# A ConvFFN's start on one core: pair sums in place, six leading products, earlier weight loads

## The chip, the cores and the metric

The kernel runs on one core of one Trainium2 chip. The metric is the device time of one execution in microseconds; of the kernel before there are three runs and one profiled execution.

## The reference

The reference is one decoder layer on a sequence of 1024 tokens of width 1024, in float32: sparse attention with a token indexer, then a gated ConvFFN, both with adaLN shift, scale and gate, and a last RMSNorm. The part that matters here:

```python
x = x + gt_m * y                                  # y: attention's output @ w_o
h = rmsnorm(x, g_ffn[i]) * (1 + sc_f) + sh_f
u, v = jnp.split(h @ w_in, 2, axis=-1)            # w_in: 1024 x 5632
u = causal_depthwise_conv(u, conv_w) + conv_b     # width 3
x = x + gt_f * ((gelu(u) * v) @ w_out)            # w_out: 2816 x 1024
```

## The kernel before, in words

TensorE (PE) multiplies in fp32r, so each operand is split into a high part (a cast on ACT) and a low part (a subtraction on DVE or POOL), `split` (L122), and each product is three matmuls, `three` (L126). The line of nearly all instructions in the profile is L89, the helper that issues them; the reader goes by tile names.

*Output projection* (L1277 to L1293, tiles `ot`, `wo`, `xt`). The attention's output, `o_sb`, lies in eight tiles of 128 tokens. In round r, `w0(r)` (L1064) transposes tile r (`ot`) and splits it (`o_h`, `o_l`); `w1(r-1)` (L1077) multiplies the tile before with the eight splits of `w_o` (48 matmuls into one accumulator of 1024 columns, `wo`), adds the result to `x` (tile `xr`, DVE), stores it (`x1d`) and normalizes it (`norm`, L221: a square on ACT, `rx` on DVE, a power on POOL, then `xn` on the engine that `NW`, L62, names). `w2a(r-2)` (L1100) transposes `xn` (`xt`) and applies the FFN's scale and shift, giving `hm`: on ACT in eight pieces for tiles 3, 6, 7 (`HM_ACT`, L64), on DVE for the others. `w2b(r-2)` (L1115) splits two of the seven combinations that the products use, `b11` and `s4` for tiles 0 to 3, `b22` and `s3` for tiles 4 to 7: a half of `hm`, and the difference `diff` of its halves (both `comb`). `W2B_DVE` (L63) names the low parts that DVE computes; POOL does the others.

In the same rounds `w_sums` (L1249) loads pairs of rows of `f_w_out` (`wb`), makes four sums and one scaling with `gt_f` on DVE (five operations of 128 x 512) and stores four results (`wt`) for the down products. `T_AT` (L69) says how many of the eleven pairs each round does.

*Up products.* Both FFN matrix products are done by halves with seven products in place of eight (`prods`, L1142 ff.). For each of 22 chunks c of 128 columns, product i = 0 to 6 has 12 matmuls of 512 columns; on the weights' side it takes a block of `f_w_in` or a sum of two blocks, on the other side `s4`, `b11` (these need tokens 0 to 511), `b22`, `s3` (tokens 512 to 1023), `s1`, `s7`, `s6` (sums of a tile of the first half and one of the second). The weights are loaded by SP (`load_up`, L1134, tile `fw`, two halves j of 512 KB per chunk), summed on POOL into one of two `ring` buffers (`prep_sum`, L1154) and split into `pr` (`prep_split`, L1164; the low part on POOL, for product 3 on DVE). `after` (L1184) combines the accumulators `m` into `u` and `v` on ACT and DVE.

*Between the two.* PSUM is first a pool of four accumulators of 1024 columns; it is closed after tile 7's `w1` (L1294), and a pool of eight accumulators of 512 columns (`banks`) takes its place. Then come tile 6's transposes, product (0,0), (0,1), tile 7's transposes, (1,0), (1,1); in between, the pair sums of s1, s7, s6 are made tile by tile (`sum_tile`, L1303, 24 sums of 128 x 256) into tiles of their own, and then split (`sum_split`, L1312, six splits of 128 x 1024).

*What sets the order.* From L559 on the program's order is a priority only: Tile's scheduler orders each engine's queue at build time by its own timing model, and an instruction that is ready goes ahead of one that is not. At run time each queue, SP's of DMAs too, is worked in that order. SBUF tiles of 4 KB a partition come from 35 slots (`NSLOT`, L29): a load or a result waits for a free one. In the loop over products `steps` (L1374) asks for sums two products ahead and splits one ahead, and `run_plan` (L1369) for the loads of chunk c + 1 at position 7c + `LOAD_AT` (L65).

Of the kernel before, what the change touches and what calls it, by code (L numbers as in the profile page):

```python
# [24 lines left out]
NF = DFF // P  # L25
# [34 lines left out]
CUT_7 = 2  # L60
FREE = "AGD"
NW = 'PDDDPPDD'  # L62
W2B_DVE = {(6, 1), (4, 1), (5, 1), (6, 0)}  # L63
HM_ACT = (3, 6, 7)  # L64
LOAD_AT = (3, 3)  # L65
UP_LOW_DVE = ((3,), (3, 6))
D_ORDER = (1, 2, 5, 6, 3, 7, 4)
D_LOAD, D_SPLIT = 16.0, 7.0
T_AT = (2, 2, 2, 1, 1, 1, 1, 1)  # L69
FIN_LAG = (1.3, 0.3)  # L70


def body(ctx, tc, a):
# [39 lines left out]
    def bank1(name):  # L113
        return bank2(name)[:, :512]
# [959 lines left out]
        ost[t] = o_h, o_l  # L1074
        split(o_h, o_l, pt.rearrange("p (k t) -> p k t", k=KD), dve)

    def w1(t):  # L1077
        o_h, o_l = ost[t]
        ps = bank2("wo")
        for j in range(2):  # L1080
            js = slice(j * 512, (j + 1) * 512)
            for k in range(KD):
                three(ps[:, js], o_h[:, k], o_l[:, k], wo[k][0][:, js], wo[k][1][:, js], k == 0, k == KD - 1)
        x1 = x_r[t]
        dve.tensor_tensor(x1, ps, x1, op=OP.add)
        nc.sync.dma_start(x1d[t], x1)
        xn1[t] = norm(x1, NW[t])

# [11 lines left out]
    def w2a(t, halves):  # L1100

        hf, o = divmod(t, 4)
        hm[t] = g = slot([P, KD, P], F, f"hm{t}")
        for k in range(KD):
            pe.transpose(halves[k // 4][:, k % 4], xn1[t][:, k * P:(k + 1) * P], ident)
        if t in HM_ACT:
            for k in range(KD):
                act.activation(g[:, k], halves[k // 4][:, k % 4], AF.Identity, bias=sh_f[:, k:k + 1], scale=a_f[:, k:k + 1])
        else:
            for i in range(2):  # L1110
                ks = slice(4 * i, 4 * i + 4)
                dve.tensor_tensor(g[:, ks], halves[i], bc(ada["a_f"][:, ks]), op=OP.mult)
            dve.tensor_tensor(g, g, bc(sh_f), op=OP.add)
# [132 lines left out]

    wt = {(i, d): dram.tile([2, P, 512], F, name=f"wt{i}_{d}") for i in range(4, 8) for d in range(ND)}

    def w_sums(q):  # L1249
        b1, b2 = [slot([P, D], F, f"wb{c}") for c in range(2)]  # L1250
        for c, b in enumerate((b1, b2)):
            nc.sync.dma_start(b, a["f_w_out"][(2 * q + c) * P:(2 * q + c + 1) * P])
        for i, o, x, y, op in ((5, b1[:, lo_t], b1[:, hi_t], b1[:, lo_t], OP.subtract),
                               (7, b1[:, hi_t], b2[:, hi_t], b1[:, hi_t], OP.subtract),
                               (6, b2[:, hi_t], b2[:, hi_t], b1[:, lo_t], OP.subtract),
# [12 lines left out]
    def on_pe(dur, f):  # L1268
# [3 lines left out]
        f()  # L1272
        clock[0] += dur

    comb_big(("b11", "s4"))
    comb_big(("b22", "s3"))
    for r in range(NT):  # L1277
        w0(r)
        if r == NT - 2:
            load_up(0, 1)  # L1280
        if r == NT - 1:
            ring = slot([P, 2, 4, P], F, "ring")
            prep_split(0, 0)
            prep_sum(0, 1)
            prep_split(0, 1)
        if r >= 1:
            w1(r - 1)
        if r >= 2:
            w2a(r - 2, [bank1("xt").rearrange("p (k t) -> p k t", k=4) for _ in range(2)])
            w2b(r - 2)  # L1290
        for q in range(sum(T_AT[:r]), sum(T_AT[:r + 1])):
            w_sums(q)
    w1(NT - 1)  # L1293
    psum_ctx.close()  # L1294
    banks = ctx.enter_context(tc.tile_pool(name="banks", bufs=8, space=bass.MemoryType.PSUM))

    def two_banks():
        return [bank("xt").rearrange("p (k t) -> p k t", k=4) for _ in range(2)]

    sums = {}  # L1300
    terms = {"s1": (0, 4), "s7": (4, 4), "s6": (0, 0)}

    def sum_tile(nm, o):  # L1303
        if o == 0:
            sums[nm] = [slot([P, 2, 512], F, f"{nm}s{i}") for i in range(2)]
        sl = slice(o * P, (o + 1) * P)
        x, y = terms[nm]
        for i in range(2):
            dve.tensor_tensor(sums[nm][i][:, :, sl], hm[o][:, x + 2 * i:x + 2 * i + 2],
                              hm[4 + o][:, y + 2 * i:y + 2 * i + 2], op=OP.add)  # L1310

    def sum_split(nm):  # L1312
        h, lo = [], []
        for i in range(2):
            h.append(slot([P, 2, 512], R, f"{nm}h{i}"))
            lo.append(slot([P, 2, 512], R, f"{nm}l{i}"))
            act.copy(h[i], sums[nm][i])
            dve.tensor_tensor(lo[i], sums[nm][i], h[i].bitcast(F), op=OP.subtract)
        comb[nm] = (lambda k: h[k // 2][:, k % 2]), (lambda k: lo[k // 2][:, k % 2])

    load_up(1, 1)
    w2a(NT - 2, two_banks())
    product(0, 0)
    load_up(0, 0)
    prep_sum(1, 1)
    prep_split(1, 0)
    w2b(NT - 2)
    prep_split(1, 1)
    prep_sum(0, 2)
    for nm in ("s1", "s7"):  # L1330
        for o in range(2):
            sum_tile(nm, o)
    product(0, 1)
    w2a(NT - 1, two_banks())
    product(1, 0)
    after(0, 1)
    w2b(NT - 1)
    prep_split(0, 2)
    prep_split(0, 3)
    prep_sum(0, 4)  # L1340
    for nm in ("s1", "s7"):
        for o in range(2, 4):
            sum_tile(nm, o)
    product(1, 1)
    sum_split("s1")
    after(1, 1)
    prep_split(0, 4)
    prep_sum(0, 5)
    for o in range(4):
        sum_tile("s6", o)  # L1350
    sum_split("s7")
    prep_split(0, 5)
    prep_sum(0, 6)
    sum_split("s6")
    prep_split(0, 6)
    seq = [(0, i) for i in range(2, 7)] + [(1, i) for i in range(2, 7)]
    seq += [(c, i) for c in range(2, NF) for i in range(7)]
    prepared = {(0, i) for i in range(7)} | {(1, 0), (1, 1)}
    summed = set(prepared)
    loaded = {(0, 0), (0, 1), (1, 1)}  # L1360

    plan = []
    for c in range(NF):
# [259 lines left out]
```

## Time and profile before

| what | value |
|---|---|
| three runs | 1184.88, 1187.29, 1187.45 us; median 1187.29 |
| the profiled execution | 1190.08 us |
| its span, first to last instruction | 1188.3 us |
| mean granted TensorE clock | 0.971 |
| output projection | about 424 to 523 us of the span |
| up products | 528 to 971 us |
| down products | to 1180 us |

Times in the profile are microseconds from the first instruction of one execution. PE is TensorE's matmuls, PEld its weight loads, DVE VectorE, ACT ScalarE, POOL GpSimd, SP the queue that issues DMAs. A row of a timeline gives start, duration, engine, operation, tiles (out<-in), shape, how many were merged, and in brackets the idle time before and what ended it.

### The profile page before, as it was taken

What the parts mean: (1) busy time and instruction counts of PE and PEld (TensorE: products, weight loads), DVE (VectorE), ACT (ScalarE), POOL (GpSimd) and SP (SyncE); (2) the same over time, 40 slices, a digit from 0 to 9 for tenths busy, and PEclk for the clock granted to TensorE, in tenths of its full rate; (3) what the DMA queues carried; (4) which work ended last, traced back from release to release, by engine and by line L of the source; (5) the groups of instructions that cost most, each with busy time, mean ns of one, the idle gap of its engine ahead of it and who ended that gap; (6) DMA issues with size and microseconds to landing.
All of it is one profiled execution on the core that took longest, in us unless ns stands there. A gap on an engine that the chain in (4) does not pass through costs nothing.

```text
span 1188.3 us, 15292 instructions
## 1 busy us (share of the span) xinstructions
PE 1108.0 (93%) x5419; PEld 914.9 (77%) x5419; DVE 897.8 (76%) x1367; ACT 540.9 (46%) x909; POOL 619.3 (52%) x379
## 2 busy tenths in 40 slices
PE   7899599869999999987999999999999999999997
PEld 6787488756777787875878887888788888888885
DVE  6867489779887659789768776887678786555587
ACT  2376578656544622334434333333334355343352
POOL 2453023032144623448989998999899840200353
PEclk8899799979999999998999999999999999999999
DMA  9633201001655579851033323323242449975351
GB/s 364 219 127 54 53 18 55 1 1 31 211 170 188 177 274 333 293 186 54 36 106 106 116 81 98 133 89 95 84 133 89 147 154 369 390 250 179 104 195 71
DMA packets 69432, 173.30 MB, mean 146 GB/s; under 512 B 6472, under 2 KB 8936, under 8 KB 69352
## 3 DMA queue, kind: packets, MB, share of 16 engines
q1 hardware_dynamic: 69208, 172.04, 42.9%
q8 instruction: 42, 0.69, 0.2%
q14 instruction: 38, 0.31, 0.1%
q10 hardware_dynamic: 144, 0.26, 0.1%
HBM read 130.59 MB, written 41.68 MB: 145 GB/s over the span
## 4 chain that ended last, share of the span: by engine, by line
PE 52%; DVE 8%; POOL 5%; DMA 5%; issue 3%; ACT 2%; SPq 0%; POOLq 0%; DVEq 0%; ACTq 0%
PE m L89 24%; PE d L89 18%; PE o L89 3%; PE wo L89 3%; DMA fw<-in_f_w_in 3%; POOL pr L89 3%; PE l L89 2%; DVE wb L89 2%; POOL ring L89 2%; PE pt L89 1%; DMA wb<-in_f_w_out 1%; DVE conv L89 1%; DVE xr L89 1%; DVE lg L89 0%; DMA ada<-in_ada_w 0%
## 5 line engine op out<-in xcount | busy, mean ns | idle before, releaser
L89 PE MATMUL m<-comb,pr 128*128 128x512 f32 x1056 | 252.3, 395 | 12.2 <-ACT comb L89 5.3
L89 PEld LDWEIGHTS m<-comb,pr 128*128 128x128 f32 x1056 | 200.4, 191 | 57.3 <-ACT pr L89 6.0
L89 PE MATMUL d<-ringb,ringa 128*128 128x512 f32 x888 | 202.1, 389 | 0.0
L89 POOL TENSOR_TENSOR pr<-ring,pr 128x512 fp32r<-128x512 f32 x108 | 190.7, 1780 | 19.6 <-ACT pr L89 19.4
L89 PEld LDWEIGHTS d<-ringb,ringa 128*128 128x128 f32 x888 | 166.7, 188 | 34.6
L89 POOL TENSOR_TENSOR ring<-fw,fw 128x512 f32<-128x512 f32 x66 | 117.4, 1791 | 1.8
L89 POOL TENSOR_TENSOR y<-y,gt_f 128x512 f32<-128x512 f32 x12 | 23.6, 1985 | 156.5 <-DVE y L89 156.5
L89 ACT CAST pr<-ring 128x512 fp32r<-128x512 f32 x110 | 66.7, 618 | 67.7 <-POOL ring L89 67.5
L89 DVE SCALAR_TENSOR_TENSOR conv<-u,small,conv 128x1023 f32<-128x1023 f32 (+1 forms) x44 | 66.8, 1518 | 28.2 <-ACT conv L89 26.8
L89 DVE TENSOR_TENSOR ringa<-da,ringa 128x1024 fp32r<-128x1024 f32 (+1 forms) x40 | 49.0, 1225 | 51.3 <-ACT ringa L89 51.1
L89 DVE TENSOR_TENSOR u<-m,u 128x512 f32<-128x512 f32 x66 | 45.3, 687 | 51.2 <-PE m L89 34.8
L89 ACT CAST ringa<-da 128x1024 fp32r<-128x1024 f32 (+1 forms) x40 | 39.6, 989 | 90.5 <-PE d L89 78.5
L89 ACT ACTIVATE lg<-lg,mx 128x128 f32<-128x128 f32 (+6 forms) x64 | 49.5, 775 | 47.8 <-DVE mx L89 47.3
L89 PEld LDWEIGHTS o<-vv,ptb 128*128 128x128 f32 x528 | 64.4, 192 | 7.5 <-issue 4.8
L89 PE MATMUL l<-kt,q 128*128 128x512 f32 (+3 forms) x160 | 66.9, 533 | 2.9 <-ACT ptb L89 1.4
L89 POOL TENSOR_TENSOR ring<-fw 128x512 f32<-128x512 f32 x44 | 61.0, 1385 | 15.8 <-DMA fw<-in_f_w_in 15.6
L89 PE MATMUL o<-vv,ptb 128*128 128x128 f32 x528 | 66.9, 276 | 0.0
L89 PE MATMUL m<-s7h,pr 128*128 128x512 f32 x176 | 58.0, 391 | 1.3 <-POOL pr L89 1.3
L89 PE MATMUL m<-s6h,pr 128*128 128x512 f32 x176 | 59.0, 396 | 0.0
L89 PE MATMUL m<-s1h,pr 128*128 128x512 f32 x176 | 58.0, 390 | 0.3 <-POOL pr L89 0.3
L89 POOL TENSOR_TENSOR mn<-near,score 128x1024 f32<-128x1024 f32 x12 | 29.8, 2487 | 51.2 <-PE pt L89 16.5
L89 ACT ACTIVATE conv<-u,small 128x1024 f32<-128x1024 f32 x22 | 27.4, 1244 | 59.3 <-DVE u L89 59.3
(294 smaller groups left out, 2591.5 us busy)
## 6 DMA issues: line engine op xcount, KB each, us to landing
fw<-in_f_w_in SPq DMA_DIRECT2D x44, 512.0 KB, 4.9
da<-ga SPq DMA_DIRECT2D x35, 512.0 KB, 6.8
ada<-in_ada_w SPq DMA_DIRECT2D x32, 512.0 KB, 3.9
wb<-in_f_w_out SPq DMA_DIRECT2D x22, 512.0 KB, 5.6
wt<-wb SPq DMA_DIRECT2D x44, 256.0 KB, 2.1
db<-wt SPq DMA_DIRECT2D x20, 512.0 KB, 9.4
ga<-conv SPq DMA_DIRECT2D x33, 256.0 KB, 2.1
db<-in_f_w_out SPq DMA_DIRECT2D x15, 512.0 KB, 6.4
```

The costliest lines, as they stand in the source:

```text
L89: r = f(*args, **kw)
```

## The change

Seven edits around the start of the FFN. Both low parts of tile 7 go from POOL to DVE (`W2B_DVE`). The eleven pairs of `f_w_out` are done in rounds 0 to 5 (`T_AT`) and loaded one round ahead (`w_load`). `w1` adds and accumulates by halves of 512 columns, tile 7's in an order by k, and the transposes of the tile before it stand in the middle of `w1(6)` and of `w1(7)`; the PSUM pools are switched before `w1(7)`, and the transposes of a tile take one accumulator of the first pool, not two. Tile 7's `hm` is half on DVE. The pair sums are made in place in `hm` (`w2c`, three sums of 128 x 512 per tile, for tiles 0 and 1 within rounds 6 and 7) and split from there tile by tile (`w2d`). Six products, (c,0) and (c,1) of chunks 0, 1 and 2, precede the first that needs tile 7, and the order after them is new (`seq`). The loads of chunk c + 1 are asked for at positions 7c - 1 and 7c (`LOAD_AT`).

```diff
--- before.py
+++ after.py
@@ -60,13 +60,13 @@
 CUT_7 = 2
 FREE = "AGD"
 NW = 'PDDDPPDD'
-W2B_DVE = {(6, 1), (4, 1), (5, 1), (6, 0)}
+W2B_DVE = {(6, 1), (4, 1), (5, 1), (6, 0), (7, 0), (7, 1)}
 HM_ACT = (3, 6, 7)
-LOAD_AT = (3, 3)
+LOAD_AT = (-1, 0)
 UP_LOW_DVE = ((3,), (3, 6))
 D_ORDER = (1, 2, 5, 6, 3, 7, 4)
 D_LOAD, D_SPLIT = 16.0, 7.0
-T_AT = (2, 2, 2, 1, 1, 1, 1, 1)
+T_AT = (2, 2, 2, 2, 2, 1)
 FIN_LAG = (1.3, 0.3)
 
 
@@ -1074,15 +1074,19 @@
         ost[t] = o_h, o_l
         split(o_h, o_l, pt.rearrange("p (k t) -> p k t", k=KD), dve)
 
-    def w1(t):
+    def w1(t, halves, between=None):
+
+
         o_h, o_l = ost[t]
-        ps = bank2("wo")
-        for j in range(2):
+        jk = [(j, k) for j in range(2) for k in range(KD)]
+        x1 = x_r[t]
+        for n, (j, k) in enumerate(sorted(jk, key=lambda e: e[1]) if t == NT - 1 else jk):
+            if between and n == KD:
+                between()
             js = slice(j * 512, (j + 1) * 512)
-            for k in range(KD):
-                three(ps[:, js], o_h[:, k], o_l[:, k], wo[k][0][:, js], wo[k][1][:, js], k == 0, k == KD - 1)
-        x1 = x_r[t]
-        dve.tensor_tensor(x1, ps, x1, op=OP.add)
+            three(halves[j], o_h[:, k], o_l[:, k], wo[k][0][:, js], wo[k][1][:, js], k == 0, k == KD - 1)
+            if k == KD - 1:
+                dve.tensor_tensor(x1[:, js], halves[j], x1[:, js], op=OP.add)
         nc.sync.dma_start(x1d[t], x1)
         xn1[t] = norm(x1, NW[t])
 
@@ -1104,7 +1108,11 @@
         for k in range(KD):
             pe.transpose(halves[k // 4][:, k % 4], xn1[t][:, k * P:(k + 1) * P], ident)
         if t in HM_ACT:
-            for k in range(KD):
+            on_dve = 4 if t == NT - 1 else 0
+            if on_dve:
+                dve.tensor_tensor(g[:, 0:4], halves[0], bc(ada["a_f"][:, 0:4]), op=OP.mult)
+                dve.tensor_tensor(g[:, 0:4], g[:, 0:4], bc(sh_f[:, 0:4]), op=OP.add)
+            for k in range(on_dve, KD):
                 act.activation(g[:, k], halves[k // 4][:, k % 4], AF.Identity, bias=sh_f[:, k:k + 1], scale=a_f[:, k:k + 1])
         else:
             for i in range(2):
@@ -1246,10 +1254,15 @@
 
     wt = {(i, d): dram.tile([2, P, 512], F, name=f"wt{i}_{d}") for i in range(4, 8) for d in range(ND)}
 
+    w_raw = {}
+
+    def w_load(q):
+        w_raw[q] = [slot([P, D], F, f"wb{c}") for c in range(2)]
+        for c, b in enumerate(w_raw[q]):
+            nc.sync.dma_start(b, a["f_w_out"][(2 * q + c) * P:(2 * q + c + 1) * P])
+
     def w_sums(q):
-        b1, b2 = [slot([P, D], F, f"wb{c}") for c in range(2)]
-        for c, b in enumerate((b1, b2)):
-            nc.sync.dma_start(b, a["f_w_out"][(2 * q + c) * P:(2 * q + c + 1) * P])
+        b1, b2 = w_raw[q]
         for i, o, x, y, op in ((5, b1[:, lo_t], b1[:, hi_t], b1[:, lo_t], OP.subtract),
                                (7, b1[:, hi_t], b2[:, hi_t], b1[:, hi_t], OP.subtract),
                                (6, b2[:, hi_t], b2[:, hi_t], b1[:, lo_t], OP.subtract),
@@ -1272,8 +1285,36 @@
         f()
         clock[0] += dur
 
+    def two_banks():
+        t = bank2("xt").rearrange("p (h k t) -> p h k t", h=2, k=4)
+        return [t[:, 0], t[:, 1]]
+
+    def w2c(o):
+
+        g0, g1 = hm[o], hm[4 + o]
+        dve.tensor_tensor(g0[:, 4:8], g0[:, 4:8], g1[:, 4:8], op=OP.add)
+        dve.tensor_tensor(g1[:, 0:4], g1[:, 0:4], g0[:, 0:4], op=OP.add)
+        dve.tensor_tensor(g0[:, 0:4], g0[:, 0:4], g1[:, 4:8], op=OP.add)
+
+    parts = {}
+
+    def w2d(nm, o):
+
+        if nm not in parts:
+            parts[nm] = h, lo = [[slot([P, 2, 512], R, f"{nm}{x}{i}") for i in range(2)] for x in "hl"]
+            comb[nm] = (lambda k: h[k // 2][:, k % 2]), (lambda k: lo[k // 2][:, k % 2])
+        h, lo = parts[nm]
+        sl = slice(o * P, (o + 1) * P)
+        t, x = {"s1": (o, 0), "s7": (o, 4), "s6": (4 + o, 0)}[nm]
+        for i in range(2):
+            src = hm[t][:, x + 2 * i:x + 2 * i + 2]
+            act.copy(h[i][:, :, sl], src)
+            dve.tensor_tensor(lo[i][:, :, sl], src, h[i][:, :, sl].bitcast(F), op=OP.subtract)
+
     comb_big(("b11", "s4"))
     comb_big(("b22", "s3"))
+    for q in range(T_AT[0]):
+        w_load(q)
     for r in range(NT):
         w0(r)
         if r == NT - 2:
@@ -1283,81 +1324,63 @@
             prep_split(0, 0)
             prep_sum(0, 1)
             prep_split(0, 1)
+            load_up(1, 1)
         if r >= 1:
-            w1(r - 1)
+            ps = bank2("wo")
+            w1(r - 1, [ps[:, :512], ps[:, 512:]], (lambda: w2a(r - 2, two_banks())) if r == NT - 1 else None)
         if r >= 2:
-            w2a(r - 2, [bank1("xt").rearrange("p (k t) -> p k t", k=4) for _ in range(2)])
+            if r < NT - 1:
+                w2a(r - 2, two_banks())
             w2b(r - 2)
         for q in range(sum(T_AT[:r]), sum(T_AT[:r + 1])):
             w_sums(q)
-    w1(NT - 1)
+        for q in range(sum(T_AT[:r + 1]), sum(T_AT[:r + 2])):
+            w_load(q)
+        if r >= 6:
+            w2c(r - 6)
     psum_ctx.close()
     banks = ctx.enter_context(tc.tile_pool(name="banks", bufs=8, space=bass.MemoryType.PSUM))
 
     def two_banks():
         return [bank("xt").rearrange("p (k t) -> p k t", k=4) for _ in range(2)]
 
-    sums = {}
-    terms = {"s1": (0, 4), "s7": (4, 4), "s6": (0, 0)}
-
-    def sum_tile(nm, o):
-        if o == 0:
-            sums[nm] = [slot([P, 2, 512], F, f"{nm}s{i}") for i in range(2)]
-        sl = slice(o * P, (o + 1) * P)
-        x, y = terms[nm]
-        for i in range(2):
-            dve.tensor_tensor(sums[nm][i][:, :, sl], hm[o][:, x + 2 * i:x + 2 * i + 2],
-                              hm[4 + o][:, y + 2 * i:y + 2 * i + 2], op=OP.add)
-
-    def sum_split(nm):
-        h, lo = [], []
-        for i in range(2):
-            h.append(slot([P, 2, 512], R, f"{nm}h{i}"))
-            lo.append(slot([P, 2, 512], R, f"{nm}l{i}"))
-            act.copy(h[i], sums[nm][i])
-            dve.tensor_tensor(lo[i], sums[nm][i], h[i].bitcast(F), op=OP.subtract)
-        comb[nm] = (lambda k: h[k // 2][:, k % 2]), (lambda k: lo[k // 2][:, k % 2])
-
-    load_up(1, 1)
-    w2a(NT - 2, two_banks())
-    product(0, 0)
+    w1(NT - 1, [bank("wo") for _ in range(2)], lambda: w2a(NT - 2, two_banks()))
+    load_up(2, 1)
     load_up(0, 0)
+    w2b(NT - 2)
     prep_sum(1, 1)
     prep_split(1, 0)
-    w2b(NT - 2)
+    w2c(2)
     prep_split(1, 1)
-    prep_sum(0, 2)
-    for nm in ("s1", "s7"):
-        for o in range(2):
-            sum_tile(nm, o)
+    load_up(1, 0)
+    product(0, 0)
     product(0, 1)
+    after(0, 1)
     w2a(NT - 1, two_banks())
     product(1, 0)
-    after(0, 1)
+    prep_split(2, 0)
+    prep_sum(2, 1)
+    prep_split(2, 1)
     w2b(NT - 1)
+    product(1, 1)
+    after(1, 1)
+    prep_sum(0, 2)
     prep_split(0, 2)
     prep_split(0, 3)
-    prep_sum(0, 4)
-    for nm in ("s1", "s7"):
-        for o in range(2, 4):
-            sum_tile(nm, o)
-    product(1, 1)
-    sum_split("s1")
-    after(1, 1)
-    prep_split(0, 4)
-    prep_sum(0, 5)
+    w2c(3)
     for o in range(4):
-        sum_tile("s6", o)
-    sum_split("s7")
-    prep_split(0, 5)
-    prep_sum(0, 6)
-    sum_split("s6")
-    prep_split(0, 6)
-    seq = [(0, i) for i in range(2, 7)] + [(1, i) for i in range(2, 7)]
-    seq += [(c, i) for c in range(2, NF) for i in range(7)]
-    prepared = {(0, i) for i in range(7)} | {(1, 0), (1, 1)}
+        w2d("s1", o)
+    product(2, 0)
+    product(2, 1)
+    after(2, 1)
+    for nm in ("s7", "s6"):
+        for o in range(4):
+            w2d(nm, o)
+    seq = [(c, i) for c in range(2) for i in (2, 3)] + [(c, i) for c in range(2) for i in (4, 5, 6)]
+    seq += [(2, i) for i in range(2, 7)] + [(c, i) for c in range(3, NF) for i in range(7)]
+    prepared = {(c, i) for c in range(3) for i in range(2)} | {(0, 2), (0, 3)}
     summed = set(prepared)
-    loaded = {(0, 0), (0, 1), (1, 1)}
+    loaded = {(c, j) for c in range(2) for j in range(2)} | {(2, 1)}
 
     plan = []
     for c in range(NF):
```

## Rows read from the trace of the kernel before

**Rows 1.** The page's first part: busy time, share of the span and instructions of each engine
```profile
PE 1108.0 (93%) x5419; PEld 914.9 (77%) x5419; DVE 897.8 (76%) x1367; ACT 540.9 (46%) x909; POOL 619.3 (52%) x379
```

**Rows 2.** Windows by stage: engines' busy us (x instructions), granted clock, DMA share, GB/s
```profile
424.00:523.20 99.20, 97.04 (x472) 80.92 (x470) 78.88 (x101) 24.80 (x42) 37.74 (x23) 1.00 0.77 278
523.20:605.00 81.80, 67.85 (x271) 53.73 (x271) 68.05 (x77) 37.40 (x62) 63.99 (x37) 0.90 0.25 85
605.00:971.50 366.50, 363.64 (x1600) 299.40 (x1599) 286.74 (x269) 143.12 (x212) 332.40 (x204) 1.00 0.34 111
971.50:1180.00 208.50, 208.50 (x921) 172.35 (x920) 138.59 (x140) 87.41 (x110) 44.44 (x30) 1.00 0.61 216
...
610.00:700.00 90.00, 90.00 (x399) 74.38 (x398) 65.97 (x65) 34.54 (x52) 82.90 (x53) 1.00 0.32 103
```

**Rows 3.** The timeline of PE, 523 to 605 us: the products that PE waited for
```profile
526.42 1.95 PE L89 MATMUL xt<-ident,xn 128*128 128x128 f32 x8 [3.01 <-DVE xr L89]
...
546.78 4.45 PE L89 MATMUL m<-comb,pr 128*128 128x512 f32 x11 [5.35 <-ACT comb L89]
...
553.47 4.36 PE L89 MATMUL m<-comb,pr 128*128 128x512 f32 x11 [2.24 <-POOL comb L89]
...
562.37 0.73 PE L89 MATMUL m<-s7h,pr 128*128 128x512 f32 x2 [1.29 <-POOL pr L89]
...
600.69 0.73 PE L89 MATMUL m<-comb,pr 128*128 128x512 f32 x2 [1.79 <-ACT pr L89]
```

**Rows 4.** Windows over the four stretches at the lower clock: one, and their sum
```profile
543.50:550.50 7.00, 3.72 (x9) 2.96 (x10) 7.00 (x15) 5.34 (x7) 3.70 (x1) 0.51 0.00 0
...
sum 17.90, PE 14.20 PEld 11.54 DVE 12.56 ACT 11.41 POOL 11.14; mean PE 3.55 PEld 2.88 DVE 3.14 ACT 2.85 POOL 2.79
```

**Rows 5.** The timeline of DVE and of ACT, tiles 6 and 7
```profile
525.15 1.22 DVE L89 TENSOR_TENSOR xr<-wo,xr 128x1024 f32<-128x1024 f32 x1
...
528.45 0.75 DVE L89 TENSOR_SCALAR xn<-xr,rxr 128x1024 f32<-128x1024 f32 x1 [0.66 <-POOL rxr L89]
...
531.82 4.72 DVE L89 TENSOR_TENSOR s1s<-hm,hm 128x256 f32<-128x256 f32 x4
...
545.39 0.68 DVE L89 TENSOR_TENSOR diff<-hm 128x512 f32<-128x512 f32 x1
...
536.96 1.54 ACT L89 ACTIVATE hm<-xt,sh_f,a_f 128x128 f32<-128x128 f32 x4
```

**Rows 6.** The timeline of POOL, 527 to 554 us
```profile
527.87 0.55 POOL L89 TENSOR_TENSOR rxr<-rx,mhalf 128x1 f32<-128x1 f32 x1 [9.24 <-DVE rx L89]
...
531.82 1.58 POOL L89 TENSOR_TENSOR ring<-fw 128x512 f32<-128x512 f32 x1 [3.40 <-DMA fw<-in_f_w_in]
...
546.80 6.61 POOL L89 TENSOR_TENSOR comb<-diff,comb 128x512 fp32r<-128x512 f32 x1 [4.56 <-ACT comb L89]
```

**Rows 7.** Instructions of tiles hm, ot and wb: duration ns min/median/max
```profile
L89 DVE TENSOR_TENSOR s1s<-hm,hm x8: 408/415/1519, 531.8 to 546.0; 128x256 f32<-128x256 f32 x8
...
L89 DVE TENSOR_TENSOR s6s<-hm,hm x8: 406/408/408, 549.5 to 551.9; 128x256 f32<-128x256 f32 x8
...
L89 DVE TENSOR_TENSOR o_l<-ot,o_h x8: 1208/1224/1225, 422.6 to 504.4; 128x1024 fp32r<-128x1024 f32 x8
...
L89 DVE TENSOR_TENSOR wb<-wb x22: 678/685/1660, 425.0 to 523.8; 128x512 f32<-128x512 f32 x22
```

**Rows 8.** The output projection: a wait of PE; windows of two stretches
```profile
448.77 0.47 PE L89 MATMUL wo<-woh,o_h 128*128 128x512 f32 x1 [1.54 <-DVE xr L89]
...
431.90:442.20 10.30, 10.30 (x47) 8.51 (x47) 2.61 (x4) 2.05 (x3) 3.43 (x2) 1.00 0.62 212
...
473.00:486.00 13.00, 13.00 (x69) 10.97 (x68) 12.57 (x16) 3.31 (x5) 4.42 (x3) 1.00 0.78 284
```

**Rows 9.** The waits of 572 to 966 us: us in total, times, longest
```profile
ACT pr L89 <- DMA fw<-in_f_w_in: 41.6, 17, 5.2
...
PE m L89 <- ACT pr L89: 4.3, 3, 1.8
```

## The prediction

> **What bounds the kernel now.** I read the page first: PE is busy 93% of the span, DVE 76%, POOL 52% [rows 1]. The averages hide the stages, so windows by stage come next [rows 2]. The output projection (424 to 523.2 us) is idle on PE for 99.20 - 97.04 = 2.2 us; the down products (971.5 to 1180) for nothing; the up products from 605 on for 366.50 - 363.64 = 2.9 us, with POOL busy 332 of 366 us, so POOL is close behind PE there. The stage between, 523.2 to 605, is the weak one: PE idles 13.95 us and the granted clock is 0.90. An undisturbed stretch (610 to 700) has 399 products in 90 us, 0.2256 us each. The weak stage holds 271 instructions, 255 of them products (57.5 us), and 16 transposes (some 2 us): 59.5 us of work in 81.8. **22.3 us are lost there.** The timeline of PE names the waits [rows 3]: 3.01 us for DVE's add of tile 7 (`xr`), 5.35 for ACT's and 2.24 for POOL's split of tile 7's difference, 1.29 for a weight split on POOL, 1.79 for one on ACT. The clock is at its lower level, 1.2 GHz, in four stretches that follow the waits of 3.01, 5.35, 2.24 and 1.79 us; in these PE is busy 14.20 us at about half pace [rows 4], which costs 7.1. The rest of the 22.3, 1.3 us, goes in restarts.
>
> Why was tile 7 late? Its `hm` was done on ACT by 536.96 + 1.54 = 538.5, but DVE's subtraction `diff` ran at 545.39, behind pair sums [rows 5]. Four of these, of 256 columns, took 4.72 us together [rows 5]: alone one takes 0.41 us, at worst 1.52 [rows 7]. The dear ones are those that meet POOL's work; an operation with one input in PSUM (`o_l`) never stretches, 1.21 to 1.23 us [rows 7]. POOL's side of the same meeting is the 6.61 us for one split, where an operation of that size took 1.58 before it [rows 6]. POOL meanwhile stood idle for 9.24 us, 3.40 (waiting for a weight load) and 4.56 us [rows 6].
>
> **The change, part by part.** T is the end of the last output product, today 523.2.
>
> *Switch of PSUM pools.* Today the transposes of tile 6, the new pool's first users, wait for tile 7's add, which DVE starts at 525.15 behind the last pair of `f_w_out`. Now the switch lies between `w1(6)` and `w1(7)`, and the add is in halves. The wait that is left is for the second half: at least 0.6 us (half of 1.22 [rows 5]), at most today's 3.01. The nearest row is the 1.54 us that a product waited for the same add [rows 8], after which the clock stayed up (1.00 in that window [rows 2]). I take 1.3.
>
> *Six products as cover.* Tile 7's add takes 0.7 us; from its end to `xn` ready took 2.83 today (526.37 to 529.20 [rows 5]): T+3.6. PE reaches tile 7's transposes after two products, T+5.4, and ends them at T+6.4. Half of `hm` is then on ACT (four pieces, 1.54 [rows 5]), half in two operations on DVE (two of 0.69 [rows 7]): T+8. Cast, subtraction, cast and two subtractions on DVE follow: 2.6 us alone, 5 when each meets POOL: T+10.6 to T+13. The first product that needs them, (0,2), comes after six products and the transposes, at T+17.2 (6 x 12 x 0.2256 + 1). The margin of 4 to 7 us covers even today's delay of `diff` (545.39 - 538.5 = 6.9) nearly. The waits of 5.35 and 2.24 and their slow stretches go; I count 0, and what is late next is POOL.
>
> *POOL's supply.* Products (2,0) and (2,1) add three POOL operations, some 5 us, ahead of (0,2). Against that stand 17 us of idleness and 5 us of the long split [rows 6], which moves to DVE with the other half of tile 7. The loads of chunks 1 and 2 are asked for earlier, but SP issues them in order, behind `x1d` stores that wait for DVE. Of 1.29 + 1.79 us and the clock behind the latter I leave 2.0 us (between 0 and 5).
>
> *Pair sums in place, splits by tile.* Out: 24 sums of 256 columns and 6 wide splits; in: 12 sums of 512 (6 of them before T) and 24 casts on ACT with 24 subtractions of 256 on DVE. The casts, at least 0.38 us each (1.54 / 4 [rows 5]), 9 us or more, lie on ACT, busy 37 of 82 us in this stage [rows 2]. Alone, DVE has 24 x 0.41 + 6 x 1.21 = 17.1 us before, 12 x 0.69 + 24 x 0.41 = 18.1 after (a 512 takes 0.69 [rows 7]); 1 us more, beside PE. Meeting POOL, each small subtraction costs 1.5. They are due from T+28 ((0,4), after ten products). Those of tiles 0 to 2 need nothing of tile 7 and can run while POOL waits. I take 4 us of waiting, nearer to the lower end, since POOL's idle stretches [rows 6] lie where these operations can start; ends 0 and 32 (worked out as a rival).
>
> The Trainium skill (SBUF — State Buffer, "SBUF: two separate sides") states that DVE with two inputs in SBUF and GpSimd exclude each other for a whole instruction; the 0.41 against 1.52 us and the steady `o_l` agree. By that rule alone all 24 pay, the slower case below. The skill's Perfetto Trace Analysis ("Optimizing Scalar/DVE Operations") gives some 60 ns of overhead per DVE operation on SBUF and advises grouping; by it 18 more operations cost 1.1 us, my estimate, while the rows here give 6 x (4 x 0.41 - 1.21) = 2.6.
>
> The stage keeps 1.3 + 2.0 + 4.0 = 7.3 us of its 22.3: **15.0 us gained.**
>
> *The output projection.* A pair of `f_w_out` costs DVE five operations of 0.69, 3.5 us. T_AT moves the pairs of rounds 6 and 7 into rounds 3 and 4. DVE was busy 12.57 of 13 us there [rows 8], so it runs 3 us over in each; queued behind it are the adds, `o_l` and `xn`, and PE waits for these. On the other side loads a round ahead use a stretch in which DVE worked 2.61 of 10.30 us [rows 8], transposes take one PSUM tile where they took two, and half of a tile's add now runs beside PE. The adds as halves cost DVE 8 x (2 x 0.69 - 1.22) = 1.3 us, beside PE. **Gain 1.0**, between 2.2 (all idle time gone) and a loss of 6. The loads and stores of a moved pair, 2 MB, come on top of a DMA share of 0.78 there [rows 8]; SP issues them between the stores of `x1d`, so they can delay those.
>
> *LOAD_AT.* Loads of chunk c+1 are issued at position 7c-1 and 7c, not 7c+3: 4 and 3 products, 11 and 8 us, earlier, for two more slots. ACT waited 41.6 us for these loads, but PE only 4.3 for ACT [rows 9], 1.79 of it counted above; 2.9 us of idleness is left after 605. **Gain 2.0** (0 to 2.9).
>
> **Sum.** 15.0 + 1.0 + 2.0 = 18.0. The profiled execution took 1190.08 us (span 1188.3 and 1.8 around it), which gives 1172.1; it is 2.8 above the median of the runs, 1187.29, so the median after is **1169 us**.
>
> **Rivals.**
> A, slower: **DVE in step with POOL.** From about T+6 POOL works without a break. In program order 12 operations on SBUF (`w2c`, `w2b(7)`, `hm`, two weight splits) and s1's 8 come first: 20 x 1.5 + 5 us on PSUM = T+41, 13 us after (0,4) is due. s7's and s6's 8 each take 12 us against 2.7 us of product: 9 us each. That is 31 us of idleness and some 5 us of clock in place of my 4: 32 lost against 18 gained, 1201. Every small subtraction done before POOL starts saves 1.5, so it decides at 12 of 24: fewer, and the kernel is slower. Half way to the full case: 1194. For it: 4.72 us for four sums. Against: the 8 sums of s6 ran at 0.41 each [rows 7]; the worst is no rule.
> B: **the projection paced by DVE.** The two overfull rounds are not absorbed: 6 us lost and the gain of 1 gone, 1169 + 7 = 1176. For: 12.57 of 13. Against: the idle stretch before it [rows 8].
> C: **the loads do not come ahead.** 35 slots are shared; sixteen hold `w_o` until T and eight `hm`, so asking earlier may issue nothing earlier, and the change would not do what it says. Then the 2.0 of LOAD_AT goes, POOL waits for chunk 2 as it waited 3.40 us [rows 6], and the supply costs 5 to 8 instead of 2: 1169 + 2 + 6 = 1177. Against: pairs of `f_w_out` leave the last rounds, which frees slots.
>
> **How the numbers follow.** Forecast 0.55, A 0.14, B 0.18, C 0.13. A measurement here tells 0.2%, 2.4 us, from no change. The forecast and nearly all of B and C are faster by more than that (0.55 + 0.16 + 0.11 = 0.82); 0.05 falls within; 0.13 is slower. The lower end: with the switch at 0.6, nothing else left in the stage, 2.2 and 2.9 from the others, 26.8 gained, 1160.5; all at once is unlikely, so 1162. The upper end takes in B, C with worse supply, and the bound of A: 1187.
>
> **What would show it.** Right: a wait of 0.6 to 1.6 us on PE at `w1(7)`'s first product and none at tile 6's transposes; six products (s4, b11) from T without a gap; `diff` of tile 7 done before T+17; no 6.6 us operation on POOL; fewer us of ACT waiting for `fw`; 523 to 605 at a clock near 1. Wrong: products of s1, s7, s6 waiting for DVE after T+28 with subtractions of 1.5 us (A); waits for `xr` or `o_l` in 450 to 500 (B); `fw` issued no earlier against its products (C). A gap elsewhere, in the down products above all, would contradict the whole account.

## The result: 0.8% slower, and the profile after

The changed kernel takes 1195.14 us (median of 8 runs, 1192.48 to 1201.56), the kernel before 1186.09 in the runs beside it: ratio 1.0079, 95% interval 1.0060 to 1.0097, some 9 us slower where 18 faster was forecast. The profiled execution took 1195.40 us (span 1193.6), 5.3 longer than that of before; the other 4 us are mostly that the profiled execution of before lay 2.8 to 4 us above its medians. The spans divide like this (us; from the first and the last row of a tile in each trace):

| stretch | before | after |
|---|---|---|
| start to the first output product (`wo`) | 422.6 | 423.3 |
| first to last output product | 100.8 | 114.1 |
| to the last up product (`m`) | 447.9 | 439.6 |
| to the last down product (`d`) | 209.2 | 209.2 |
| rest | 7.8 | 7.4 |

The FFN's start gained 8.3 us, and the output projection lost 13.3. By the page's first part the averages hardly differ from [rows 1]:

```profile
PE 1110.1 (93%) x5419; PEld 914.7 (77%) x5419; DVE 894.5 (75%) x1385; ACT 540.1 (45%) x923; POOL 608.6 (51%) x377
```

The windows by stage of the changed kernel (columns as in [rows 2]) show where the time is, and the last row the end of the projection at a lower clock:

```profile
423.30:537.40 114.10, 103.81 (x492) 83.95 (x491) 87.09 (x120) 29.43 (x52) 39.29 (x24) 0.99 0.71 256
537.40:620.00 82.60, 71.15 (x289) 55.76 (x289) 68.00 (x83) 35.57 (x69) 58.99 (x37) 0.94 0.25 80
620.00:977.00 357.00, 356.30 (x1572) 294.84 (x1571) 278.48 (x266) 140.20 (x209) 324.69 (x201) 1.00 0.33 111
977.00:1186.20 209.20, 209.20 (x922) 172.67 (x920) 139.34 (x140) 87.42 (x110) 44.42 (x30) 1.00 0.62 217
508.40:537.40 29.00, 26.06 (x116) 20.88 (x114) 17.77 (x24) 9.43 (x20) 15.76 (x9) 0.94 0.15 55
```

PE now idles 114.10 - 103.81 = 10.3 us in the projection, where it idled 2.2 [rows 2]. The timeline of PE there names the waits:

```profile
432.21 0.50 PE L89 MATMUL wo<-woh,o_h 128*128 128x512 f32 x1 [1.71 <-DVE xr L89]
...
445.19 0.51 PE L89 MATMUL wo<-woh,o_h 128*128 128x512 f32 x1 [0.78 <-DVE xr L89]
...
460.34 0.50 PE L89 MATMUL wo<-woh,o_h 128*128 128x512 f32 x1 [0.41 <-DVE xr L89]
...
472.59 1.09 PE L89 MATMUL xt<-ident,xn 128*128 128x128 f32 x8 [1.08 <-DVE xn L89]
...
474.87 0.50 PE L89 MATMUL wo<-woh,o_h 128*128 128x512 f32 x1 [0.31 <-DVE xr L89]
...
487.31 1.09 PE L89 MATMUL xt<-ident,xn 128*128 128x128 f32 x8 [1.23 <-DVE xn L89]
...
501.10 0.51 PE L89 MATMUL wo<-woh,o_h 128*128 128x512 f32 x1 [0.82 <-DVE xr L89]
...
514.43 1.09 PE L89 MATMUL xt<-ident,xn 128*128 128x128 f32 x8 [0.34 <-POOL xn L89]
517.24 0.80 PE L89 MATMUL wo<-woh,o_h 128*128 128x512 f32 x1 [1.72 <-DVE xr L89]
...
525.35 0.47 PE L89 MATMUL wo<-woh,o_h 128*128 128x512 f32 x1 [0.88 <-DVE xr L89]
```

Count the products between two such rows: the waits for `xr` stand after the 24th product of a tile, not after the 48th. At 432.21, 445.19, 460.34, 474.87, 501.10 and 517.24 PE wants to begin the second half of tiles 0, 1, 2, 3, 5 and 6, and waits until DVE has added the first: 5.75 us. In the gaps of tiles 3, 4 and 6 stand transposes, which wait for `xn` themselves (2.65 us); tile 4 has no wait for `xr` behind them. Two waits for `o_l` take 1.02, and the switch of PSUM pools, the last row, 0.88: 10.3 in all. That is 8.1 us more idleness than before. The other 5 us of the 13.3 are mostly tile 6's transposes, which moved in (0.9), restarts (the first product after a wait takes 0.50 us, others 0.39), and slow clock behind the 1.72 (the 24 products there took 7.24 us, those behind the 0.82 took 5.70).

After T (now 537.4) the waits of 5.35, 2.24 and 3.01 us [rows 3] are gone, and these stand in their place:

```profile
544.64 1.09 PE L89 MATMUL xt<-ident,xn 128*128 128x128 f32 x8 [1.82 <-DVE xn L89]
...
558.81 4.85 PE L89 MATMUL m<-comb,pr 128*128 128x512 f32 x20 [1.24 <-DVE pr L89]
565.19 0.73 PE L89 MATMUL m<-comb,pr 128*128 128x512 f32 x2 [1.52 <-ACT pr L89]
...
568.59 3.96 PE L89 MATMUL m<-comb,pr 128*128 128x512 f32 x10 [1.67 <-POOL pr L89]
...
613.31 11.33 PE L89 MATMUL m<-comb,pr 128*128 128x512 f32 x36 [4.08 <-ACT pr L89]
```

The timelines of POOL, ACT and DVE show two in-order queues behind them. ACT casts for s7 and s6, sixteen in a row (5.1 us), and POOL stands 8.20 us for a cast of `pr` queued behind them:

```profile
565.21 3.32 POOL L89 TENSOR_TENSOR pr<-ring,pr 128x512 fp32r<-128x512 f32 x1 [8.20 <-ACT pr L89]
...
559.61 2.55 ACT L89 CAST s7h<-hm 128x256 fp32r<-128x256 f32 x8
562.06 2.55 ACT L89 CAST s6h<-hm 128x256 fp32r<-128x256 f32 x8
564.52 0.61 ACT L89 CAST pr<-ring 128x512 fp32r<-128x512 f32 x1
...
564.65 2.76 DVE L89 TENSOR_TENSOR s6l<-hm,s6h 128x256 fp32r<-128x256 f32 x8
```

Some 40 us later DVE has the first four sums for the down products (`sa`, `sb`), three of them at 1.6 to 1.8 us beside POOL, ahead of `u` and `v` of chunk 2; ACT's `conv` of chunk 2 waits 11.27 us for `u`, and the casts of chunk 3 wait behind it:

```profile
602.17 1.59 DVE L89 TENSOR_TENSOR sa<-conv 128x512 f32<-128x512 f32 x1
603.68 1.77 DVE L89 TENSOR_TENSOR sb<-conv 128x512 f32<-128x512 f32 x1
605.38 1.77 DVE L89 TENSOR_TENSOR sa<-sa,conv 128x512 f32<-128x512 f32 x1
607.08 0.68 DVE L89 TENSOR_TENSOR u<-m,u 128x512 f32<-128x512 f32 x1
...
611.51 1.24 ACT L89 ACTIVATE conv<-u,small 128x1024 f32<-128x1024 f32 x1 [11.27 <-DVE u L89]
612.65 1.12 ACT L89 CAST pr<-ring 128x512 fp32r<-128x512 f32 x2
```

### The profile page after: what moved, and what is told of

Its sections match the earlier page's. It is cut to its first block, busy times and chain, and to the rows that moved or that the text cites. A ratio compares the mean times of both kernels' runs of the same rounds, so it can differ in the third digit from the quotient of the medians.

```text
span 1193.6 us, 15343 instructions
## 1 busy us (share of the span) xinstructions
PE 1110.1 (93%) x5419; PEld 914.7 (77%) x5419; DVE 894.5 (75%) x1385; ACT 540.1 (45%) x923; POOL 608.6 (51%) x377
## 4 chain that ended last, share of the span: by engine, by line
PE 56%; DVE 8%; issue 3%; POOL 3%; DMA 2%; ACT 2%; SPq 0%; POOLq 0%; DVEq 0%; ACTq 0%
PE m L89 28%; PE d L89 18%; PE o L89 3%; PE wo L89 3%; PE l L89 2%; POOL pr L89 2%; PE pt L89 1%; DVE wb L89 1%; DMA wb<-in_f_w_out 1%; DVE hm L89 1%; DVE conv L89 1%; POOL xn L89 1%; POOL ring L89 1%; DMA ada<-in_ada_w 1%; DVE u L89 0%
## 5 line engine op out<-in xcount | busy, mean ns | idle before, releaser
L89 PE MATMUL wo<-woh,o_h 128*128 128x512 f32 x128 | 51.8, 405 | 6.6 <-DVE xr L89 6.6
```

The source lines that it names most:

```text
L89: r = f(*args, **kw)
```

## The experiments

All were timed in five rounds beside the kernel before. In the readings "projection" is first to last output product and "up stretch" from there to the last up product, of one profiled execution.

**Halves, pairs, casts, loads: one edit each on the changed kernel.** In `e1_own`:

```diff
-            ps = bank2("wo")
-            w1(r - 1, [ps[:, :512], ps[:, 512:]], (lambda: w2a(r - 2, two_banks())) if r == NT - 1 else None)
+            w1(r - 1, [bank1("wo") for _ in range(2)], (lambda: w2a(r - 2, two_banks())) if r == NT - 1 else None)
```

> The changed kernel, with the two halves of a tile's accumulator in the output projection as two PSUM tiles of their own in place of two views of one tile. The adds stay halves, the pairs of f_w_out stay where they are. Theory 1, the halves: the first product of a second half writes the tile that DVE's add of the first half reads, so TensorE waits for that add in the middle of tiles 0 to 6 (5.75 us of waits for xr in the changed kernel, and restarts and low clock behind them). Then the waits for xr in the middle of a tile vanish, the projection from its first to its last product takes 103 to 107 us in place of 114.1, and the ratio to the kernel before falls from 1.008 to 0.998 to 1.002. Theory 2, DVE overfull with five rounds of two pairs: the waits only move to o_l and xn, the projection stays at 111 us or more, ratio 1.005 to 1.009.

In `e2_tat`:

```diff
-T_AT = (2, 2, 2, 2, 2, 1)
+T_AT = (2, 2, 2, 1, 1, 1, 1, 1)
```

> The changed kernel with the pairs of f_w_out spread over all eight rounds as before (2, 2, 2, 1, 1, 1, 1, 1); halves in one tile as in the change. Theory 1 (the halves): the waits for xr in the middle of the tiles stay, at 4 us or more, the projection stays above 110 us, ratio 1.004 to 1.009. Theory 2 (DVE overfull): the projection falls to 101 to 104 us, ratio 0.996 to 1.000.

Measured: `e1_own` 1.0020 (1.0005 to 1.0036), projection 108.6 us, no wait in the middle of a tile; `e2_tat` 1.0086 (1.0062 to 1.0110), projection 115.4, all six waits still there and a seventh in tile 4, 7.69 us in sum. So the wait is between the halves, as theory 1 has it: with two views of one tile the second half's product waits for the reader of the first, with two tiles it does not. The projection came down less than expected. What is left in PE's timeline of `e1_own` are waits at a tile's start:

```profile
464.44 0.47 PE L89 MATMUL wo<-woh,o_h 128*128 128x512 f32 x1 [0.67 <-DVE xr L89]
466.08 0.51 PE L89 MATMUL wo<-woh,o_l 128*128 128x512 f32 x1 [0.94 <-DVE o_l L89]
...
520.51 0.47 PE L89 MATMUL wo<-woh,o_h 128*128 128x512 f32 x1 [1.56 <-DVE xr L89]
```

In `e3_late` (w2d of s7 and s6 in the loop over products):

```diff
-    for nm in ("s7", "s6"):
-        for o in range(4):
-            w2d(nm, o)
...
+        if p in (1, 2):
+            for o in range(4):
+                w2d(("s7", "s6")[p - 1], o)
```

> The changed kernel with the sixteen small splits of s7 and s6 issued after the second and the third product of the order behind the six, so that they stand on ACT's queue behind the casts of products (1,2) and (1,3). Theory: in the changed kernel POOL idled 8.20 us behind ACT's casts of s7 and s6, and TensorE then waited 1.52, 0.27 and 1.67 us for weight splits. Then the 8.20 falls below 3, these three waits fall below 1.5 in sum, and the kernel gains 2 to 5 us on the changed one: ratio 1.004 to 1.006. Rival: what is late there is DVE, with small subtractions in step with POOL; then the waits come back as waits for the low parts of s1, s7, s6, and the ratio stays at 1.007 to 1.009.

Measured: 1.0083 (1.0059 to 1.0106). The 8.20 us of POOL became 3.29 and the three waits of PE went, but a wait of 6.57 us took their place (timelines of PE and DVE of `e3_late`):

```profile
578.53 0.79 PE L89 MATMUL m<-s6l,pr 128*128 128x512 f32 x1 [6.57 <-DVE s6l L89]
...
572.80 6.35 DVE L89 TENSOR_TENSOR s6l<-hm,s6h 128x256 fp32r<-128x256 f32 x6
```

The rival holds: four of the six subtractions in this row began while an operation of POOL ran, the two engines took turns, and these four cost 1.5 us each, where the changed kernel has 2.76 for eight. ACT's block of casts had kept POOL still and so DVE cheap; the two costs exchange. Meeting POOL is not by itself dear for DVE, though. In the changed kernel POOL's split of 565.21 came into the run of s6's subtractions: the six that were left took 0.41 us each, and the split took 3.32. In the kernel before it was the same: the operation of 6.61 us on POOL [rows 6] ran beside s6's sums of 0.41 [rows 7].

In `e4_load`:

```diff
-LOAD_AT = (-1, 0)
+LOAD_AT = (3, 3)
```

> The changed kernel with the weight loads asked for at position 7c + 3 as before. Theory: the earlier request is what removed the waits of 0.97, 1.57 and 0.32 us that TensorE had between 700 and 965 us; without it they come back, some 3 us with the restarts, ratio 1.009 to 1.012. Rival: the loads were held by other things (slots, stores ahead of them), and asking earlier did nothing: no new waits after 620 us, ratio 1.007 to 1.009.

Measured: 1.0073 (1.0050 to 1.0095), the rival's ratio, not to be told from the changed kernel. Two small waits came back (0.52 us at 839, 0.73 at 960), where the changed kernel has none from 613 to 967, and in the waits of 572 to 966 us ACT's for `fw`, absent from the changed kernel there, is back:

```profile
ACT pr L89 <- DMA fw<-in_f_w_in: 36.1, 17, 4.1
```

So the mechanism is as the theory says, but its size is some 1.3 us by the two waits, not 3; the timing can't tell it.

**What else the projection loses.** `e6_whole` gives tiles 0 to 6 one add again:

```diff
-            if k == KD - 1:
+            if k == KD - 1 and t == NT - 1:
                 dve.tensor_tensor(x1[:, js], halves[j], x1[:, js], op=OP.add)
+        if t < NT - 1:
+            dve.tensor_tensor(x1, wo_ps[0], x1, op=OP.add)
```

> The changed kernel with one add of 1024 columns per tile after all 48 products for tiles 0 to 6, as before; tile 7 stays in halves, the pairs stay in five tiles and are loaded a round ahead. Theory: the wait in the middle of a tile costs some 8 us of the 13.3 that the projection grew by, and the accumulators of halves of their own (the first experiment) gave some of that back because they took a fourth accumulator per round and left the transposes of the next tile no lead. Then the projection takes 102 to 105 us (114.1 in the changed kernel, 108.6 with halves of their own), and the ratio is 0.994 to 0.999. Rival: the loads a round ahead hold slots and delay o_h and o_l; then it stays at 107 us or more, with waits for o_l, ratio above 1.000.

`e7_whole_direct` has, besides, the loads in the round of the sums; `e9_direct` has that alone:

```diff
-        for q in range(sum(T_AT[:r + 1]), sum(T_AT[:r + 2])):
-            w_load(q)
...
+            w_load(q)
             w_sums(q)
```

> As the one above, and the pairs of f_w_out loaded in the round that sums them, as before. If the loads ahead cost anything, this one is faster than the one above by what they cost: the rival expects 3 to 6 us, the theory 0 to 1.

> The changed kernel with the halves in one tile and the pairs loaded in the round that sums them, as before. The theory (halves) expects the waits in the middle of the tiles as in the change: projection 111 to 114 us, ratio 1.005 to 1.008. The rival (slots held by loads ahead) expects 106 to 109 us, ratio 1.000 to 1.004.

`e8_old_proj` is the one with one add and direct loads, with the pairs over eight rounds and two accumulators for a tile's transposes, as before:

> The projection of the kernel before for tiles 0 to 6 (one add, two accumulators for a tile's transposes, pairs over eight rounds, loaded directly), tile 7 and all that follows as in the change. It shows what the second half of the change is worth alone: the stretch from the last output product to the last up product took 447.9 us before and 439.6 after, so the sum is 7 to 9 us faster than before, ratio 0.992 to 0.995. The rival that the up products gained only because the projection gave DVE and the loads more time beforehand: 445 us or more for that stretch, ratio 0.997 or above.

Measured: 1.0026 (1.0005 to 1.0048), 1.0028 (1.0015 to 1.0041), 1.0106 (1.0083 to 1.0129) and 1.0025 (1.0010 to 1.0040); projections 110.9, 107.9, 120.5 and 109.7 us. One add cures the middle of the tiles as well as separate accumulators do, and no more. Loading ahead makes no clear difference in the times: with one add 1.0026 and 1.0028, with halves 1.0079 and 1.0106, whose intervals overlap. In the traces the direct loads are 3 us shorter with one add, where most of the waits for `o_l` of `e6_whole` (3.9 us) are gone, as the rival had it, and 6.4 us longer with halves; the runs don't settle it. The lengths expected were all too short. The up stretch of `e8_old_proj`, 440.9 us, is near the 439.6 of the changed kernel, so its rival fell; its theory's ratio was missed in the projection, 109.7 us with the old form of tiles 0 to 6, where the kernel before has 100.8 (this profiled execution lay 4.4 us above its median). In `e7_whole_direct` and `e8_old_proj` the largest wait is the switch of pools, which now lies inside the projection, and DVE comes late there (in `e6_whole` it waits 1.68 us, in `e9_direct` 0.88). PE's timeline of `e7_whole_direct` at the switch:

```profile
517.60 0.47 PE L89 MATMUL wo<-woh,o_h 128*128 128x512 f32 x1 [3.81 <-DVE xr L89]
```

And that of `e8_old_proj`:

```profile
520.82 0.77 PE L89 MATMUL wo<-woh,o_h 128*128 128x512 f32 x1 [5.42 <-DVE xr L89]
```

The switch was to be cheap; with the old projection it costs 5.42 us, more than the 3.01 before [rows 3]. It is 0.88 in every run with the halves as views of one tile, where PE has been held in the middle of tile 6 just before, and 1.5 to 5.4 in every run without them. I take the one to be the reason for the other; no run separates them.

**The queue before the switch.** Two tries, on `e7_whole_direct`. `e10_sums_later` issues `w2c` of tiles 0 and 1 behind the switch; `e12_t6` gives, besides, tile 6 accumulators of its own and two adds.

> One add per tile and direct loads of the pairs (the seventh experiment), and the pair sums of tiles 0 and 1 after the switch of PSUM pools in place of rounds 6 and 7. Theory: DVE's queue ahead of tile 6's add (pair sums, a low part, a pair of f_w_out, drawn out by POOL's work beside them) makes the switch wait 3.81 us; with six operations fewer it waits 1.0 to 2.2 us, the projection falls from 107.9 to 104.5 to 106.5 us and the ratio from 1.003 to 0.999 to 1.001. Rival: the six operations are only moved behind the switch and cost the same there: the stretch from the last output product to the last up product grows from 438.2 by 2 us or more, ratio 1.002 to 1.004.

> As the one above, with tile 6 in two accumulators of its own and two adds. Theory: half of the add then runs beside TensorE and nothing writes what it reads; the wait at the switch is at most 1.0 us and there is none in the middle of tile 6: 0.5 to 1.5 us less than the one above. Rival: DVE's queue and not the size of the add sets the switch; no difference.

Measured: 1.0030 (1.0017 to 1.0042) and 1.0058 (1.0042 to 1.0075). `e10_sums_later` tested nothing: the scheduler put the three sums of tile 0 at the same place, 506 to 514 us, since they were ready, and the wait stayed at 3.81. In `e12_t6` the switch waits 5.13 us: the second half's add ran at 523.16, 4.3 us after its products, behind five other operations of DVE. The theory fell; the rival is right that DVE's queue sets the switch, but the kernel became slower than `e10_sums_later`, not equal. `e18_late3`, below, is the test that bites.

**The late sums.** `e14_s67` issues the splits of s7 and s6 after the second product of the order; `e13_asum` has, besides:

```diff
-                    later(LATER[1], lambda: a_sums(q))
+                    later(LATER[1] + (14.0 if q == 0 else 0.0), lambda: a_sums(q))
```

In the next text the first that it names is `e10_sums_later`, and the third experiment `e3_late`:

> As the first of this call, with the sixteen splits of s7 and s6 issued after the second product of the order (the third experiment had s6 one product later, where DVE's subtractions fell in step with POOL and a product waited 6.57 us for s6l). Theory: ACT then casts for products (1,2) and (1,3) first, POOL does not stand for 8 us, and DVE still has most of the subtractions done before POOL is busy: the waits for pr in 555 to 575 us fall from 3.5 us in sum to under 1.5, none over 1 us for s7l or s6l; 2 to 4 us less than the first of this call. Rival: the small subtractions meet POOL and a product waits for s6l by 3 us or more; no gain.

> As the one above, and the first four sums for the down products (sa, sb of chunks 0 and 1) issued 14 us later. Theory: the wait of 4.08 us for ACT some 85 us after the switch comes from DVE's queue: these four sums, 1.6 to 1.8 us each beside POOL, stand ahead of u and v of chunk 2, ACT's conv of chunk 2 waits for u (11.27 us in the changed kernel), and the casts of chunk 3 wait behind that conv. With them later the 4.08 falls below 1.0 and the kernel gains 3 to 5 us with the restart and the slow clock behind it. Rival: the wait is POOL's lead being used up by the loads of chunk 3, which came at 591 to 614 us: it stays above 3 us.

Measured: 1.0020 (1.0007 to 1.0033) and 0.9962 (0.9948 to 0.9975). `e14_s67` gains nothing that the intervals tell (one wait of 2.42 us for `pr` of POOL remains there; none for `s7l` or `s6l`). `e13_asum` takes the wait of 4.01 us out whole, and the slow stretch behind it; the up stretch falls from 437.4 to 431.2 us. The window of `e13_asum` over chunk 2's `conv` (601.6) and the sums (now from 610) has PE busy throughout, at a clock of 1.00:

```profile
597.00:617.00 20.00, 20.00 (x90) 16.54 (x89) 18.55 (x17) 7.41 (x11) 18.00 (x11) 1.00 0.39 131
```

The same place in the changed kernel:

```profile
609.00:619.00 10.00, 5.92 (x15) 4.48 (x14) 9.22 (x9) 3.85 (x5) 5.67 (x3) 0.68 0.42 131
```

**One cause or two.** The late sums on the changed kernel alone (`e15_asum_only`), and with the halves in tiles of their own (`e16_own_asum`):

> The changed kernel with one edit: the first four sums for the down products 14 us later. If the two causes are independent, the wait of 4.08 us at 613 us goes here too, with 2 us of slow clock behind it, the projection stays at 112 to 115 us, and the ratio to the kernel before falls from 1.008 to 1.001 to 1.004. Rival: the gain of the last run hung on the sixteen splits moved with it; then the wait stays or moves, ratio 1.006 or more.

> The changed kernel with both cures: the halves in accumulators of their own, and the four sums 14 us later. If the two causes add up, the ratio is 0.995 to 0.998 (1.002 with the first alone, less 0.005 to 0.006). If they are one cause (DVE's lateness carried on from the projection), it stays at 1.000 or above.

Measured: 1.0016 (1.0004 to 1.0028) and 0.9978 (0.9965 to 0.9992). The wait of 4.08 us is gone from both (the projection of `e15_asum_only` is 116.5 us, above the 115 expected, in an execution 5.8 us above its median). The late sums are worth 0.0063 by themselves, the halves 0.0059; from 1.0079 the two add up to 0.9957, and 0.9978 was found, which the intervals just allow. They are two causes; a small part in common is not excluded. Why the sums are dear only after the change stays open: in the kernel before the same four stand ahead of chunk 2's `u` too (DVE, 590.13 to 596.83, `u` from 596.75), but there ACT has the next weight cast (600.01) ahead of chunk 2's `conv` (600.65), and the wait of 1.79 us [rows 3] behind that cast came from its load.

**DVE's load.** On `e13_asum`, one pair of `f_w_out` goes to chunk 5 (`e17_late1`), or three to chunks 5, 8 and 11 (`e18_late3`, `T_AT = (2, 2, 2, 1, 1)`):

> The fastest so far (one add per tile, direct loads, splits and sums later) with the eleventh pair of f_w_out in chunk 5 of the up products. Theory: part of this pair's operations stand ahead of tile 6's add and hold the switch of pools by 3.8 us; without them the wait is 1.0 to 2.5 us, with 1 us of slow clock, ratio 0.993 to 0.996. Rival: the rest of DVE's queue (tile 5's hm, low parts beside POOL) fills the place; no difference, 0.995 to 0.998.

> As the one above with three pairs of f_w_out (chunks 5, 8 and 11), eight in five rounds of the projection. If DVE's load is what is left of the projection's loss, 10 us less of it bring the projection from 109 to 104 to 106 us, ratio 0.989 to 0.994. Rival: what is left is the order of the queues; 0.994 to 0.998; and where the pairs come late, DVE's operations beside POOL can cost waits of 1 us there.

Measured: 0.9969 (0.9954 to 0.9983) and 1.0001 (0.9988 to 1.0013). The projection fell from 109.2 to 105.2 and to 100.8 us. In `e13_asum` DVE works without a gap before the switch:

```profile
510.00:521.00 11.00, 7.30 (x37) 5.89 (x35) 10.97 (x12) 1.30 (x4) 8.32 (x5) 1.00 0.26 89
```

With three pairs fewer (`e18_late3`) PE waits only once in the whole projection, at the switch:

```profile
511.71 0.47 PE L89 MATMUL wo<-woh,o_h 128*128 128x512 f32 x1 [1.68 <-DVE xr L89]
```

A pair brings its loads and stores along, too. But DVE's waits for the loads of pairs are alike in the two projections, 3.6 and 3.5 us, while its busy time is 88.8 and 75.0 us (80.4 in the kernel before). So DVE's load is the rest of the projection's loss. But the pairs cost the same or more where they went: the up stretch grew from 431.2 to 435.6 and 444.5 us, and the ratios came out with the rival (`e17_late1`) or above both (`e18_late3`). The waits of PE in 620 to 965 us (us in total, times, longest), in `e13_asum`:

```profile
PE m L89 <- POOL pr L89: 0.7, 1, 0.7
```

And with three pairs there, in `e18_late3`:

```profile
PE m L89 <- ACT pr L89: 6.5, 5, 2.6
PE m L89 <- POOL pr L89: 1.8, 6, 0.7
```

The fastest version is `e13_asum`, 0.9962 of the kernel before and some 1.2% under the changed one.

## Why the prediction was wrong, step by step

- *Output projection, "gain 1.0", and "half of a tile's add now runs beside PE"*: the step that failed. I took the halves for independent. They are views of one tile, so PE has to wait in the middle of tiles 0 to 6 for the half that was to be hidden; undoing that gave back 0.53% to 0.59%, 6 to 7 us, twice (`e6_whole`, `e1_own`). The projection lost 13.3 us where 1.0 was to be gained: 3 to 6 of these are the halves by the traces (107.9 to 110.9 us without them), and the rest, some 8, DVE's load (next point). The bound of -6 was for DVE's load and not for the halves.
- *Rival B*: its place was right (the projection paced by DVE), its first waits were not. T_AT alone gained nothing (`e2_tat`): the mid-tile waits stayed. With them gone DVE's load shows as the wait at the switch, and three pairs less bring the projection back to 100.8 us. The load was not T_AT's alone: tile 6's transposes and the pair sums of tiles 0 and 1 moved in as well, and with the pairs spread as before (`e8_old_proj`) the projection is still 109.7.
- *Switch, 1.3 us*: 0.88 measured, but only in the shadow of the mid-tile wait; 1.53 to 5.42 without. The 1.54 of [rows 8] was too kind a neighbour, since pairs, sums and a low part stand ahead of that add.
- *Cover of six products, 0 us*: the waits of 5.35 and 2.24 us went, as said. Tile 7's transposes waited 1.82 for `xn`, which I had not counted, and its last low part was ready at 555.86, T+18.5, not T+13: DVE ran the five operations up to it at 1.75 to 1.78 us. The margin was used up. Behind the same operations DVE made a weight's low part at 558.08, and PE waited 1.24 us for it, which stands in no term.
- *POOL's supply, 2.0 left*: 1.52 + 0.27 + 1.67 + 0.66 = 4.1 us of waits for `pr`, inside the 0 to 5. The cause of the first three was not loads but ACT's casts, which I had taken for free (`e3_late` is without them), and the 6.6 us operation did go (no operation of POOL over 3.32 in its place).
- *Small splits, 4 us*: none in the changed kernel. POOL stood still for most of them, but behind ACT's casts and not in the idle stretches of [rows 6]; for the last six POOL paid, so that "all 24 pay" is too strong. `e3_late` shows rival A's price, 1.5 us each and 6.57 us of waiting, where DVE and POOL take turns. A's "12 of 24" leaves out the 4 us already in the sum: 1201 less 1187 is 14 us, 9 or 10 subtractions.
- *LOAD_AT, 2.0*: ACT's 41.6 us of waiting for `fw` [rows 9] are gone from the changed kernel's waits of 572 to 966 us, and `e4_load` brings 36.1 back; worth some 1.3 us by the trace, as PE seldom waited for them. Rival C fell.
- *Left out*: what comes later. Two chunks end together after the new order, and their four sums stand ahead of chunk 2's `u`, `conv` and the casts of chunk 3: 6.2 us of the up stretch. With that removed the up stretch is 431.2 us against 447.9, a gain of 16.7 where 17.0 had been forecast. But 3.9 of it, the switch's 3.01 and tile 6's transposes, only moved into the projection, so the route is not the one forecast.

The rule of the Trainium skill (SBUF — State Buffer, "SBUF: two separate sides") that DVE with two inputs in SBUF and GpSimd keep each other out for a whole instruction agrees with the traces at each of these places: 0.41 us for a subtraction of 256 columns alone, 1.5 where it began during one of POOL's operations; 0.68 and 1.75 for 512.

## What to carry to other kernels

When an accumulator is read by halves, give each half a tile of its own, and look for the wait of the second half's first write on the first half's reader; one read after both is the other cure. A new order of work must be followed until the old rhythm is back: operations that become due early (here four sums that nobody needs soon) can stand in an in-order queue ahead of urgent ones. Moving work off a full engine in one stage only pays if the stage that receives it has that engine free, contention with its neighbours counted.

## What the runs showed that was not expected

A wait can make its neighbours cheap: while POOL was held for 8.20 us, 18 of the 24 subtractions began at 0.41 us each, the other six kept that pace at POOL's cost, and with PE held in the middle of tile 6 the switch cost 0.88 in place of 1.53 to 5.42. And moving an instruction in program order need not move it on its engine: an instruction that is ready is queued where it was, as `e10_sums_later` did, without effect.
